# A hybrid attention and ConvFFN layer: TensorE's instructions of the attention stage in written order

## The chip, the cores and the metric

The kernel runs on one core of one Trainium2 chip. The metric is the device time of one execution in microseconds (us). The engines are named as the profile names them: PE is TensorE's matmuls, PEld its weight loads (they overlap the matmuls), DVE is VectorE, ACT is ScalarE, POOL is GpSimd, SP is SyncE, whose queue issues most of the loads.

## The reference

One layer over 256 tokens of width 2048, all in float32. `h @ w_in` gives queries, keys and values for two groups of eight heads of width 128. Eight heads are "forgetting attention" (FoX): normed queries and keys, a softmax over logits with a cumulative forget bias. Eight are "stick-breaking" (SB): weights from a running sum of log-sigmoids. Both results are normed, multiplied by `w_out` and added to x. Then comes an FFN: an up-projection to 2 x 5632 columns, a causal convolution of width 3, a SiLU gate, a down-projection.

```python
def reference(x, attn_norm, w_in, b_forget, q_norm, k_norm, out_norm_fox, out_norm_sb,
              w_out, ffn_norm, w_up, conv_w, conv_b, w_down):
    for layer in range(DEPTH):                       # DEPTH is 1
        h = rms_norm(x, attn_norm[layer])
        x = x + hybrid_mixer(h, w_in[layer], b_forget[layer], q_norm[layer], k_norm[layer],
                             out_norm_fox[layer], out_norm_sb[layer], w_out[layer])
        h = rms_norm(x, ffn_norm[layer])
        x = x + conv_ffn(h, w_up[layer], conv_w[layer], conv_b[layer], w_down[layer])
    return x

# forgetting_attention, per block of queries
        logits = jnp.einsum('bhqd,bhkd->bhqk', qi.astype(jnp.float32), k32) * scale
        logits = logits + ci[..., None] - c32[:, :, None, :]
        ...
        p = jax.nn.softmax(logits, axis=-1)
        return jnp.einsum('bhqk,bhkd->bhqd', p.astype(v.dtype), v)
```

## The kernel before

The arithmetic is float32 made of parts. Each weight tile of 128 x 2048 numbers (1 MB) is loaded into `w_raw` on SP's queue, cast to a rounded part `w_hi` by ACT (L207) and reduced to the rest `w_lo` by DVE (L208, which needs ACT's cast first). Activations are split in the same manner. A product then is three: hi by hi, lo by hi, hi by lo.

In the attention stage the projections to queries, keys and FoX values are cut into weight blocks of four 128-row tiles by up to 512 columns. One block is 24 matmuls in `in_three` (L229): 16 that use `w_hi`, then 8 that use `w_lo`. `w_hi` and `w_lo` have two buffers each in this stage, so that the cast for a block can start when the `w_hi` matmuls of the block two before it have ended, and its `w_lo` split when that block's `w_lo` matmuls have ended.

The heads are Python generators that are advanced by `step()` once after each weight block, at most two heads at a time (`WINDOW = 2`). A FoX head (`fox_head`, L611) goes through these phases:

- four score matmuls into the PSUM tile `ps_s` (L617, L518), then on DVE the bias (L624), the mask (L628) and the row maxima (L630, L631), on ACT the two exponentials (L633, L634), on DVE the reciprocal (L636) and the factors (L637, L638) that make `pr` the softmax weights
- two yields, so two weight blocks, later: `transposed_weights`, three transposes on TensorE into `ps_p` (L603), copied and split by ACT (L606, L607) and DVE (L608) into `pT`
- one yield later: `weighted`, four matmuls into `ps_o` (L589, L590), split into `oT` by ACT (L353) and DVE (L354), with sums of squares (L358, L361, L362)

`ps_s` and `ps_p` share two PSUM buffers. The SB heads are built alike. Queries and keys of four FoX heads pass through `fox_rows`: ACT scales them to `raw` (L298), DVE norms them (L323 to L328), and after one or more yields `to_heads` transposes them into `ps_h` (L304).

What sets the order of instructions: everything inside the attention stage is recorded in the order in which the program writes it, and then a list scheduler, with its own estimates and with priorities (weight loads and splits are written under `high_priority(offset=AHEAD)`), fixes an order for every engine. Two pieces are exempt: the opening (`opening`, the first projection, L473 to L476) and the FFN (from L1090) stand under `tc.manual_schedule`, in which the engines named keep the written order. In both kernels each engine executes its fixed list from front to back, and semaphores hold an instruction until its inputs are there.

The place that matters below is the stretch of the stage in which heads 0 to 3 run beside the last weight block of the queries of heads 4 to 7 (`project(512, 512)`, L648) and the four blocks of their keys (`project(WF + 512 * half, 512)`, L653). The other place is the transpose `pp` of the parameter rows (L128) in `columns(pcol, prow, 50)` (L481), with the small product `gq` (L489) that follows on DVE.

Of the kernel before, what the change touches and what calls it, by code (L numbers as in the profile page):

```python
# [45 lines left out]
def hybrid_layer(  # L46
# [49 lines left out]
    def load_parameters(masks):  # L96
        r0 = KT
        for src, n in (
            (ffn_norm, KT), (out_norm_fox, NH), (out_norm_sb, NH), (q_norm, 1), (k_norm, 1)
        ):  # L100
            nc.sync.dma_start(prow[r0 : r0 + n, :], src[0].rearrange("(n p) -> n p", p=P))
            r0 += n
        nc.sync.dma_start(cs[:, P:], cst[:, P:C_MF])
        nc.sync.dma_start(masks, cst[:, C_MF:])
        nc.sync.dma_start(bf, b_forget.to_broadcast([P, NH]))
# [178 lines left out]
    with ExitStack() as actx:  # L284
# [188 lines left out]
        with tc.high_priority(offset=AHEAD), tc.manual_schedule(  # L473
            engines={mybir.EngineType.PE, mybir.EngineType.DVE, mybir.EngineType.Activation, mybir.EngineType.SP}
        ):
            acc_q0 = opening()  # L476
        masks = at.tile([P, 2 * P], F32, name="masks")
        load_parameters(masks)
        rstd1, _ = token_factors(ss1, 1, diagonal=False)
# [592 lines left out]
    for f_lo, f_hi in FFN_PARTS:  # L1072
# [11 lines left out]
        for g in ORDER if f_hi < NFT else LAST_ORDER:  # L1084
# [7 lines left out]
            engines={mybir.EngineType.PE, mybir.EngineType.DVE, mybir.EngineType.Activation, mybir.EngineType.SP, mybir.EngineType.Pool}  # L1092
# [73 lines left out]
```

## Time and profile before

| | us |
|---|---|
| median of 3 runs | 1104.37 (1104.33 to 1104.72) |
| the profiled execution | 1103.89 |
| its span, first to last instruction | 1102.1 |
| TensorE busy | 1097.4 |
| TensorE weight loads busy | 951.2 |
| DVE busy | 877.1 |
| ACT busy | 700.8 |
| POOL busy | 44.4 |

The granted clock of TensorE is 1.000 over the whole span.

How the rows below are read. A row of the timeline has the start in us, the time from the start of the first to the end of the last instruction of the row, the engine, the line, the operation, the output and inputs, the shape, the count, and in brackets the engine's idle time before it with the instruction that ended it. A row of the waits has the waiting engine and line, what it waited for, the total in us, the times, and the longest. A row of the windows has the stretch, its length, and then for PE, PEld, DVE, ACT and POOL the busy time and the number of instructions, and at the end the granted clock, the share in which the DMA engines were busy and their GB/s. The modelled end of a matmul lies behind the start of the next, so that a group's length is read best from start to start.

### The profile page before, as it was taken

Reading aid. Unit: us, or ns where it says so; the run is one execution under the profiler, and the core shown is the slowest. Engines: PE = TensorE matmul, PEld = TensorE weight load, DVE = VectorE, ACT = ScalarE, POOL = GpSimd, SP = SyncE. Lnnn points to the kernel's source line nnn. Section 1 sums busy time; section 2 is a strip of 40 time slices with the busy share of each in tenths; the row PEclk is TensorE's granted clock in tenths of the full one; section 3 lists DMA queues with packets and bytes.
Section 4 is the critical chain, followed back from the end, with each engine's and each line's share of the span. In section 5 each row is a group of like instructions: output and inputs, shape, how many; then the busy total and the mean of one; then the engine's idle time right before and its main releaser. Section 6 shows DMA issues by size and latency. Waiting matters only on the chain.

```text
span 1102.1 us, 14836 instructions
## 1 busy us (share of the span) xinstructions
PE 1097.4 (100%) x5868; PEld 951.2 (86%) x5868; DVE 877.1 (80%) x941; ACT 700.8 (64%) x879; POOL 44.4 (4%) x46
## 2 busy tenths in 40 slices
PE   9999999999999999999999999999999999999998
PEld 7998888888888888888888888888888888888887
DVE  6656877875775677689889988889798889889896
ACT  6544565664553567667767776767676677667753
POOL 0000000000000000000000010100000010100010
PEclk9999999999999999999999999999999999999999
DMA  8776555475555396558989597987979688987985
GB/s 288 185 233 230 188 154 159 148 253 182 176 168 186 105 326 201 187 170 214 283 229 305 191 238 263 262 267 178 319 207 305 215 219 277 248 265 196 323 213 168
DMA packets 179407, 245.89 MB, mean 223 GB/s; under 512 B 4432, under 2 KB 119018, under 8 KB 179082
## 3 DMA queue, kind: packets, MB, share of 16 engines
q1 hardware_dynamic: 162458, 209.67, 58.4%
q0 software_dynamic: 16560, 34.75, 16.7%
q8 instruction: 46, 0.75, 0.3%
q10 hardware_dynamic: 320, 0.53, 0.1%
q14 instruction: 23, 0.19, 0.0%
HBM read 242.82 MB, written 2.11 MB: 222 GB/s over the span
## 4 chain that ended last, share of the span: by engine, by line
PE 99%; ACT 0%; DVE 0%; issue 0%
PE pu L256 34%; PE acc L229 22%; PE pu L263 18%; PE bank_a L229 10%; PE bank_b L229 5%; PE bank_c L229 2%; PE acc L425 2%; PE acc L1044 1%; PE ps_x L138 1%; PE ps_o L589 1%; PE bank_a L1044 1%; PE ps_p L603 0%; PE ps_o L590 0%; PE ps_h L304 0%; PE idle L378 0%; PE ps_z L518 0%
## 5 line engine op out<-in xcount | busy, mean ns | idle before, releaser
L208 DVE TENSOR_TENSOR w_lo<-w_raw,w_hi 128x2048 fp32r<-128x2048 f32 (+1 forms) x196 | 439.7, 2246 | 148.0 <-ACT w_hi L207 146.8
L207 ACT CAST w_hi<-w_raw 128x2048 fp32r<-128x2048 f32 (+1 forms) x196 | 367.2, 1876 | 265.8 <-PE pu L256 77.1
L256 PE MATMUL pu<-hT,w_hi 128*128 128x512 f32 x1664 | 396.3, 390 | 0.0
L256 PEld LDWEIGHTS pu<-hT,w_hi 128*128 128x128 f32 x1664 | 309.6, 188 | 62.6
L263 PEld LDWEIGHTS pu<-hT,w_lo 128*128 128x128 f32 x1664 | 213.6, 191 | 8.3
L263 PE MATMUL pu<-hT,w_lo 128*128 128x256 f32 x1664 | 216.2, 283 | 0.0
L229 PE MATMUL acc<-w_hi,hT 128*128 128x512 f32 (+1 forms) x576 | 124.9, 368 | 0.0
L229 PEld LDWEIGHTS acc<-w_hi,hT 128*128 128x128 f32 x576 | 101.3, 188 | 14.1
L207 ACT CAST w_hi<-w_sum 128x2048 fp32r<-128x2048 f32 x30 | 57.3, 1909 | 42.8 <-PE pu L256 36.6
L208 DVE TENSOR_TENSOR w_lo<-w_sum,w_hi 128x2048 fp32r<-128x2048 f32 x30 | 68.7, 2290 | 19.3 <-ACT w_hi L207 19.3
L866 ACT ACTIVATE tap<-up,ccol 128x256 f32<-128x256 f32 x176 | 74.6, 495 | 0.0
L229 PE MATMUL acc<-w_lo,hT 128*128 128x512 f32 (+1 forms) x288 | 64.9, 367 | 0.0
L229 PEld LDWEIGHTS acc<-w_lo,hT 128*128 128x128 f32 x288 | 51.6, 188 | 7.4
L971 POOL DMA_DIRECT2D w_sum<-in_w_down_dram x20 | 25.7, 1285 | 796.7 <-DVE w_lo L208 786.1
L229 PE MATMUL acc<-w_hi,oT 128*128 128x512 f32 x192 | 46.0, 392 | 0.0
L229 PEld LDWEIGHTS acc<-w_hi,oT 128*128 128x128 f32 x192 | 35.7, 188 | 7.3
L229 PE MATMUL bank_a<-w_hi,s 128*128 128x512 f32 x160 | 40.1, 392 | 0.1
L229 PE MATMUL bank_b<-w_hi,s 128*128 128x512 f32 x160 | 40.0, 392 | 0.0
L229 PE MATMUL bank_a<-w_hi,g 128*128 128x512 f32 x160 | 40.0, 392 | 0.0
L229 PEld LDWEIGHTS bank_a<-w_hi,s 128*128 128x128 f32 x160 | 28.8, 189 | 5.7 <-issue 0.5
L229 PEld LDWEIGHTS bank_a<-w_hi,g 128*128 128x128 f32 x160 | 28.9, 189 | 5.2
L229 PEld LDWEIGHTS bank_b<-w_hi,s 128*128 128x128 f32 x160 | 28.9, 189 | 5.3
(211 smaller groups left out, 1068.9 us busy)
## 6 DMA issues: line engine op xcount, KB each, us to landing
w_raw<-in_w_up_dram SPq DMA_DIRECT2D x88, 1024.0 KB, 7.6
w_raw<-in_w_down_dram SPq DMA_DIRECT2D x44, 1024.0 KB, 6.5
w_raw<-in_w_in_dram SPq DMA_DIRECT2D x36, 1024.0 KB, 5.3
w_sum<-in_w_down_dram POOLq DMA_DIRECT2D x20, 1024.0 KB, 10.0
w_raw<-in_w_out_dram SPq DMA_DIRECT2D x16, 1024.0 KB, 5.1
w_raw<-in_w_down_dram POOLq DMA_DIRECT2D x10, 1024.0 KB, 14.8
w_raw<-in_w_in_dram SPq DMA_DIRECT2D x12, 688.0 KB, 4.1
w_raw<-in_w_in_dram SPq DMA_DIRECT2D x6, 512.0 KB, 7.7
```

Source lines behind the costliest of these rows:

```text
L138: nc.tensor.transpose(ps[:, j, t * P : (t + 1) * P], xt[t][:, (k + j) * P : (k + j + 1) * P], ident)
L207: act.copy(hi[:, :n], raw[:, :n])
L208: dve.tensor_tensor(lo[:, :n], raw[:, :n], f32(hi[:, :n]), op=ALU.subtract)
L229: nc.tensor.matmul(o, lhs(i, l, t), r[:, i, :], start=starts and j == 0, stop=stops and j == 3 * n - 1, skip_group_check=more,)
L256: nc.tensor.matmul(acc[:, j, :], hi[:, i, j * P : (j + 1) * P], hT[:, k].rearrange("p a b -> p (a b)"), start=k == 0, stop=False,)
L263: nc.tensor.matmul(acc[:, j, S:], lo[:, i, j * P : (j + 1) * P], hT[:, k, 0, :], start=False, stop=k == KT - 1,)
L425: nc.tensor.matmul(acc[:, t, :], of_half(hT[:, 2 * c + i + j], l, t), r[:, j, :], start=high and c == i == m == 0, stop=not high and c == ...
L589: nc.tensor.matmul(po, v[j][:, hs], wp[:, k], start=i == 0, stop=False)
L866: act.activation(taps[w][:, j, :], u[:, j, w : w + S], AF.Copy, scale=ccol[:, w, f : f + 1])
L971: nc.gpsimd.dma_start(mem[into][:, : nk * 512].rearrange("p (a b) -> p a b", a=nk), src, accum_op=ALU.add)
L1044: nc.tensor.matmul(o, of_half(g, l, t), r[:, i, c0 : c0 + cols], start=kh == 0 and j == 0, stop=kh == n - 1 and j == 11,)
```

## The change

One line is added behind the opening. It enters `tc.manual_schedule` for TensorE alone and keeps it until the attention stage closes.

```diff
@@ -474,6 +474,7 @@
             engines={mybir.EngineType.PE, mybir.EngineType.DVE, mybir.EngineType.Activation, mybir.EngineType.SP}
         ):
             acc_q0 = opening()
+        actx.enter_context(tc.manual_schedule(engines={mybir.EngineType.PE}))
         masks = at.tile([P, 2 * P], F32, name="masks")
         load_parameters(masks)
         rstd1, _ = token_factors(ss1, 1, diagonal=False)
```

What TensorE does behind that line keeps the written order among itself, and the scheduler orders the other engines around it. Line numbers behind L476 are one higher in the changed kernel. In the two built programs TensorE's list differs in two places. The transpose `pp` stands behind three instead of two matmuls of the opening's eighth block. And in the stretch named above, where A is the last block of the queries of heads 4 to 7 and B to E are the blocks of their keys:

```
before                                    after
A: 16 w_hi, 8 w_lo                        A: 16 w_hi, 8 w_lo
B: 16 w_hi                                6 ps_p (heads 0 and 1)
1 ps_p                                    B: 16 w_hi, 8 w_lo
B: 1 w_lo                                 8 ps_o (heads 0 and 1)
5 ps_p                                    8 ps_s (heads 2 and 3)
B: 7 w_lo                                 C: 16 w_hi, 8 w_lo
1 ps_o, C: 2 w_hi, 1 ps_o, C: 10 w_hi     8 ps_h
the other 6 ps_o mixed with 8 ps_s        D: 16 w_hi, 8 w_lo
C: 4 w_hi, 8 w_lo                         6 ps_p (heads 2 and 3)
8 ps_h                                    E: 16 w_hi, 8 w_lo
D, 6 ps_p, E
```

ACT's list differs in that stretch alone: the four copies out of `ps_p` (L606, L607 before) now precede the cast for D, and the exponentials of head 2 precede the cast for E. DVE's list differs there too: the two splits of `pT` and the norming of the keys precede the `w_lo` split for D, and some of the work on heads 2 and 3 precedes the split for E. Beside the moved `pp`, DVE's `gq` product stands two instructions later. The lists of POOL and SP are the same.

## The prediction

> **What bounds the kernel now.** I read the page's busy shares and its chain first, then the list of waits of the two TensorE rows (PE matmuls, PEld weight loads), and last the timeline of the one place where the built program of the changed kernel differs.
>
> ```profile
> span 1102.1 us, 14836 instructions
> PE 1097.4 (100%) x5868; PEld 951.2 (86%) x5868; DVE 877.1 (80%) x941; ACT 700.8 (64%) x879; POOL 44.4 (4%) x46
> PE 99%; ACT 0%; DVE 0%; issue 0%
> ```
>
> TensorE is busy for 1097.4 of 1102.1 us and holds 99% of the chain that ends last: a microsecond in which it stands still is a microsecond on the end, unless a later wait of its own gets shorter. So the second view is what there is to get shorter.
>
> ```profile
> PE idle L378 <- DVE zeros L368: 1.1, 1, 1.1
> PE acc L425 <- ACT hT L143: 0.3, 1, 0.3
> ...
> PEld bank_a L229 <- issue: 0.5, 1, 0.5
> ...
> PEld ps_p L603 <- DVE pr L637: 0.3, 1, 0.3
> PEld ps_o L589 <- DVE pT L608: 0.2, 1, 0.2
> PEld ps_o L589 <- ACT pT L606: 0.2, 1, 0.2
> ```
>
> Of TensorE's waits two lie in the opening, before the stage that is changed; behind the changed place only the 0.5 us of bank_a is left. Three small ones (ps_p, ps_o) lie at the changed place itself. The kernel has nothing to win beyond fractions of a microsecond there, and no slack behind it to absorb a loss. DVE and ACT matter only through what they hand to TensorE.
>
> **The change, part by part.** Nothing is computed anew; instructions change places. By the order in which the two built programs stand, TensorE's list differs at two places, DVE's and ACT's at the same two (the scheduler fits them to it), POOL's and SP's queues not at all, so no transfer moves.
>
> First place, near 29 us: the transpose of the parameter rows (pp) stands one 128x512 matmul later, and on DVE the tiny gq product two instructions later.
>
> ```profile
> 28.99 0.26 PE L128 MATMUL pp<-cs,prow 50*128 50x50 f32 x1
> ```
>
> Its reader on DVE copies 50 columns and the next weight split queues behind that copy, one matmul (0.23 us, below) later. TensorE's stream holds the same instructions in either order, so I take nothing; the bounds are 0 and 0.23 us. If that split's cover were gone it would cost those 0.23 us.
>
> Second place, 124 to 136 us, is the case. Call the five weight blocks around it A to E (24 matmuls each: 16 with w_hi, 8 with w_lo): A starts at 118.68 us and ends the queries of FoX heads 4 to 7, B to E are the keys of those heads.
>
> ```profile
> 122.35 1.98 PE L229 MATMUL acc<-w_lo,hT 128*128 128x512 f32 x8
> 124.16 3.79 PE L229 MATMUL acc<-w_hi,hT 128*128 128x512 f32 x16
> 127.81 0.33 PE L603 MATMUL ps_p<-cs,pr 128*128 128x128 f32 x1
> 127.89 0.48 PE L229 MATMUL acc<-w_lo,hT 128*128 128x512 f32 x1
> 128.21 0.76 PE L603 MATMUL ps_p<-cs,pr 128*128 128x128 f32 x5
> 128.72 1.87 PE L229 MATMUL acc<-w_lo,hT 128*128 128x512 f32 x7
> ...
> 138.36 1.03 PE L304 MATMUL ps_h<-cs,raw 128*128 128x128 f32 x8
> ```
>
> Before, the scheduler lets B's 16 w_hi matmuls (124.16 to 127.81) go ahead of the six transposes of the softmax weights of heads 0 and 1 (ps_p, L603), and scatters the products ps_o among B's end and C. In program order all six transposes stand directly behind A, then B whole, then all eight ps_o matmuls and all eight score matmuls ps_s of heads 2 and 3, then C whole. TensorE would reach the first transpose at 124.16 us. When is its input there?
>
> ```profile
> 122.59 1.91 ACT L207 CAST w_hi<-w_raw 128x2048 fp32r<-128x2048 f32 x1
> ...
> 125.29 0.50 ACT L634 ACTIVATE pr<-pr,nm 128x256 f32<-128x256 f32 x1
> ```
>
> ```profile
> 124.54 2.29 DVE L208 TENSOR_TENSOR w_lo<-w_raw,w_hi 128x2048 fp32r<-128x2048 f32 x1 [1.25 <-ACT w_hi L207]
> 126.75 0.22 DVE L636 RECIPROCAL rl<-l 128x2 f32<-128x2 f32 x2
> 126.88 0.67 DVE L323 TENSOR_TENSOR sq<-raw 128x512 f32<-128x512 f32 x1
> 127.47 0.28 DVE L637 TENSOR_SCALAR pr<-pr,rl 128x128 f32<-128x128 f32 x1
> 127.67 0.35 DVE L638 TENSOR_SCALAR pr<-pr,rl 128x256 f32<-128x256 f32 x1
> 127.93 0.28 DVE L637 TENSOR_SCALAR pr<-pr,rl 128x128 f32<-128x128 f32 x1
> 128.12 0.35 DVE L638 TENSOR_SCALAR pr<-pr,rl 128x256 f32<-128x256 f32 x1
> ```
>
> The last factor is applied at 127.47 to 128.47 us (L637, L638), behind a weight split of 2.29 us that itself waited for ACT's cast. Up to these four instructions the order of DVE and of ACT from 30 us on is the same in both programs, and nothing in it waits for B. So the inputs come when they came: the first transpose starts at 127.81, the sixth follows head 1's last factor, and the next matmul starts at 128.72, as before. The difference is what is left to do at 128.72: before, seven w_lo matmuls of B; now, all 24 of B.
>
> The sum, from the start of B before (124.16) to the start of E before (145.28), by stretches of the trace:
>
> ```profile
> 117.53:118.68 1.15, 1.15 (x11) 1.15 (x10) 0.82 (x1) 0.29 (x1) 0.00 (x0) 1.00 0.55 210
> 118.68:124.16 5.48, 5.48 (x26) 4.51 (x25) 4.57 (x11) 2.06 (x3) 0.00 (x0) 1.00 0.52 166
> 124.16:145.28 21.12, 21.12 (x114) 17.54 (x112) 19.40 (x48) 14.54 (x35) 0.00 (x0) 1.00 0.50 152
> 139.15:144.71 5.56, 5.56 (x28) 4.54 (x27) 4.58 (x11) 4.16 (x9) 0.00 (x0) 1.00 0.46 132
> 144.71:145.28 0.57, 0.57 (x8) 0.57 (x6) 0.25 (x1) 0.34 (x2) 0.00 (x0) 1.00 1.08 370
> 150.85:151.93 1.08, 1.08 (x11) 1.07 (x10) 0.70 (x1) 1.08 (x3) 0.00 (x0) 1.00 1.04 361
> ```
>
> Each stretch is one undisturbed group: 1.15 us for eight ps_s, 5.48 for a block (0.23 a matmul), 5.56 for D, 0.57 for six ps_p, 1.08 for eight ps_o; the eight ps_h take 0.79 (138.36 to 139.15). Work after: from 128.72 on B 5.48 + ps_o 1.08 + ps_s 1.15 + C 5.48 + ps_h 0.79 + D 5.56 + ps_p 0.57 = 20.11, so E starts at 148.83 instead of 145.28: **3.55 us later**. The same seen as waits: 124.16 to 128.72 is 4.56 us for transposes of 0.57, a stall of 3.99; the scattered order before lost 21.12 - (20.11 + 0.57) = 0.44 us to its small waits, which the program order wins back.
>
> Does a second wait follow? The queue behind the waiting transposes is all of TensorE; what waits for it is the freeing of weight buffers, thus the splits for D and E on ACT and DVE, and behind DVE's split the chain of heads 2 and 3.
>
> ```profile
> 134.73 0.48 DVE L354 SCALAR_TENSOR_TENSOR oT<-ps_o,pcol,oT 128x256 fp32r<-128x256 f32 x1
> ...
> 136.13 0.73 DVE L624 SCALAR_TENSOR_TENSOR pr<-minus_c,c_of,ps_s 128x128 f32<-128x128 f32 x2
> ...
> 143.49 0.35 DVE L638 TENSOR_SCALAR pr<-pr,rl 128x256 f32<-128x256 f32 x1
> ```
>
> B's w_hi part ends at 128.72 + 3.79 = 132.51; ACT's cast for D (1.91) ends at 134.42, DVE's split (2.29) at 136.71, two oT instructions (0.48 each) at 137.67. From first score add to last factor the chain of heads 2 and 3 took 136.13 to 143.84, 7.71 us with E's split in it; from 137.67 it ends at 145.38. TensorE wants it at 148.83 - 0.57 = 148.26: 2.9 us of cover. D wants its split at 142.7 and has it at 136.7. Behind E the orders are equal, so I take nothing more. If this cover were gone, the cost is its overrun; I bound it by 1 us.
>
> The profiled execution took 1103.89 us, 1.79 outside its span; the median of the runs is 1104.37, 0.48 above it. 1104.37 + 3.55 = **1107.9 us**, slower by 0.32%.
>
> **Rivals.** *The stall makes TensorE slow.* Between A's last matmul (122.35 + 1.98 = 124.33) and the first transpose lie 3.48 us of silence, 4.39 up to B's first matmul. What a TensorE does that comes out of idleness is seen at the kernel's start:
>
> ```profile
> 2.73 1.06 PE L378 MATMUL idle<-zeros 128*128 128x256 bf16 x4
> 5.03 0.60 PE L378 MATMUL idle<-zeros 128*128 128x256 bf16 x4
> L378 PE MATMUL idle<-zeros x18: 272/421/421, 1.1 to 5.4; 128*128 128x256 bf16 x18
> 2.00:3.00 1.00, 1.00 (x7) 0.69 (x6) 0.00 (x0) 0.50 (x1) 0.00 (x0) 1.00 0.71 201
> ```
>
> The same matmul of zeros first comes every (1.06 - 0.42) / 3 = 0.21 us, and every (0.60 - 0.27) / 3 = 0.11 us from 5.03 us on: half speed for some 3.9 us after the first at 1.1, while the granted clock reads 1.00. If the silence brings that back, B's first 3.9 us do half their work and 2.0 us are added: 1109.9. [...] Against it: the silence is barely as long as the half-speed stretch at the start, and no later row of the list of waits is long enough to show it. [...] I give it 0.17.
>
> *The other side: no change.* If the factors were there when TensorE comes, at 124.16, the program order would even win its 0.44 us: 1103.9. The mechanism would be DVE taking the reciprocals and factors ahead of the split at 124.54. It decides from a first factor 2 us earlier than 127.47, where the loss falls under 2.2 us. But the exponentials end on ACT only at 125.79, and the built program keeps the split first. I give 0.07 to this and to a TensorE that does not keep the written order, and 0.03 to a gain of over 0.2% from anything unseen.
>
> *A second stall.* The cover of 2.9 us for heads 2 and 3 is worked out, not seen. An overrun of up to 1 us gives 1108.9. I give it 0.05.
>
> **How the numbers follow.** 0.2% of the median, 2.2 us, is about what a measurement of this kernel can tell from no change. Forecast 0.68 (its own range 1107.4 to 1108.4: 3.55 less the 0.5 us of bank_a that a later wait might give back, or plus the 0.44 if the small waits stay), slow TensorE 0.17, second stall 0.05: slower 0.90. No change 0.07, faster 0.03. The range goes from 1107.2, the forecast's lower bound and 0.2 for the profiled row against the median, to 1110.0, which takes in the half-speed case; it leaves out the 0.10 below.
>
> **What would show it.** In the profile after: the list of waits gets one row of about 3.6 us for the weight loads or matmuls of ps_p on DVE's pr, at 124 to 128 us, once, and the ps_o waits go. B's first matmul starts near 128.7, C's near 136.4, E's near 148.8, and every later block some 3.5 us later than before, to a span near 1105.6. ps_p of heads 2 and 3 shows no wait. Half speed would show as B's matmuls every 0.46 us for up to 3.9 us instead of 0.23. The prediction is wrong if the first transpose starts well before 127.8, if B runs slowly, or if a wait over 0.5 us stands anywhere behind E that is not there now.

## The result

| | before | after |
|---|---|---|
| median of 6 runs each, us | 1104.31 (1104.0 to 1104.72) | 1109.22 (1108.26 to 1110.43) |
| the profiled execution, us | 1103.89 | 1110.43 |
| its span, us | 1102.1 | 1108.6 |

The changed kernel is slower by 4.9 us: a ratio of 1.0045 with a 95% interval of 1.0035 to 1.0055. The forecast was 1107.9 us, the range 1107.2 to 1110.0. Its direction, place and main term hold. The forecast took TensorE at full speed behind the wait, and that did not come true: the granted clock over the span is 0.998 in each of the six runs, where the profiled execution of the kernel before has 1.000.

The profiled execution is the slowest of the six, so its 6.5 us over the span before are more than the median's 4.9. First the list of waits of TensorE's matmuls in the changed kernel (what waited for what; total, times, longest in us), whose line numbers are one higher than before:

```profile
PE ps_p L604 <- DVE pr L638: 3.5, 1, 3.5
PE bank_a L229 <- ACT w_hi L207: 1.1, 1, 1.1
PE idle L378 <- DVE zeros L368: 1.1, 1, 1.1
PE acc L425 <- DVE w_hi L406: 0.7, 1, 0.7
```

The row of 3.5 us is the predicted one. The small waits on ps_o are gone. The others are not the change's: acc lies in the opening at 6 us (0.3 before), and bank_a lies at 1086 us in the last FFN part; over the executions traced for this study it varies from nothing to 1.8 us, and it is 0.9 us in a run below whose time equals the kernel before.

The timeline of the place in TensorE's matmuls, with the end of A, the transposes, B and the start of E:

```profile
119.20 3.83 PE L229 MATMUL acc<-w_hi,hT 128*128 128x512 f32 x16
122.86 1.98 PE L229 MATMUL acc<-w_lo,hT 128*128 128x512 f32 x8
128.31 1.59 PE L604 MATMUL ps_p<-cs,pr 128*128 128x128 f32 x6 [3.48 <-DVE pr L638]
129.56 4.71 PE L229 MATMUL acc<-w_hi,hT 128*128 128x512 f32 x16
134.11 1.98 PE L229 MATMUL acc<-w_lo,hT 128*128 128x512 f32 x8
...
150.06 0.82 PE L604 MATMUL ps_p<-cs,pr 128*128 128x128 f32 x6
150.63 3.92 PE L229 MATMUL acc<-w_hi,hT 128*128 128x512 f32 x16
```

A starts 0.52 us later than before (119.20 against 118.68, from the opening). From the start of A to the start of E it is 31.43 us against 145.28 - 118.68 = 26.60 before: 4.83 us are lost here. The rest to 6.5 is the 0.52 ahead of A and 1.1 on bank_a. Of the rows, the transposes take 129.56 - 128.31 = 1.25 us where 0.91 was forecast from the row before, and B's w_hi part takes 134.11 - 129.56 = 4.55 us where it took 3.65 (3.75 in the kernel with the silence filled, below). The stretches of that time show why; the third number from the right is the granted clock:

```profile
126.00:127.00 1.00, 0.00 (x0) 0.00 (x0) 1.00 (x1) 1.00 (x4) 0.00 (x0) 1.00 0.00 0
127.00:128.00 1.00, 0.00 (x0) 0.00 (x0) 1.00 (x5) 0.54 (x1) 0.00 (x0) 0.93 0.00 0
128.00:129.00 1.00, 0.69 (x3) 0.61 (x4) 1.00 (x6) 0.00 (x0) 0.00 (x0) 0.50 0.67 84
...
130.00:131.00 1.00, 1.00 (x4) 0.71 (x4) 1.00 (x4) 0.79 (x4) 0.00 (x0) 0.50 1.08 385
131.00:132.00 1.00, 1.00 (x5) 0.87 (x4) 0.97 (x7) 0.21 (x2) 0.00 (x0) 0.87 0.96 329
132.00:133.00 1.00, 1.00 (x6) 0.79 (x6) 0.93 (x4) 0.20 (x1) 0.00 (x0) 1.00 0.02 6
```

The clock is halved from about 127.86 us on, still in the silence, to about 131.26 us. In a mean of 0.93 over 1 us, 2 x 0.07 = 0.14 us are at half speed; with 3 us at 0.50 and 2 x 0.13 = 0.26 that makes 3.40 us, of which 2.95 lie behind the first transpose. DVE's first factor for these transposes (first row below) came when it was forecast, 8.78 us behind A's start (8.79 before), and the next chain, of heads 2 and 3 (second row), had cover:

```profile
127.98 0.28 DVE L638 TENSOR_SCALAR pr<-pr,rl 128x128 f32<-128x128 f32 x1
...
147.18 0.35 DVE L639 TENSOR_SCALAR pr<-pr,rl 128x256 f32<-128x256 f32 x1
```

The second row ended at 147.53 and was wanted at 150.06: 2.5 us, where 2.9 were worked out.

### The profile page after: what moved, and what is told of

The parts are those of the page before. It is cut to its first block, busy times and chain, and to the rows that moved or that the text cites. A ratio compares the mean times of both kernels' runs of the same rounds, so it can differ in the third digit from the quotient of the medians.

```text
span 1108.6 us, 14836 instructions
## 1 busy us (share of the span) xinstructions
PE 1099.0 (99%) x5868; PEld 952.6 (86%) x5868; DVE 877.1 (79%) x941; ACT 701.2 (63%) x879; POOL 44.4 (4%) x46
```

## The experiments

All kernels keep the changed kernel's line unless their edit says otherwise. Times are compared with runs of the kernel before that were taken beside them: 1104.94 us for the first four, 1104.20 us for the next four, 1104.84 us (one run) for the last four. The granted clock is known for every run, the timeline for the profiled one alone.

**The silence filled.** In `fox_head`, ahead of the transposes:

```diff
             yield
             yield
+            if h == 0:
+                fill = psb.tile([P, S], F32, name="fill", tag="t")
+                for _ in range(28):
+                    nc.tensor.matmul(fill, zeros[:, :P], zeros, start=True, stop=True)
             w = transposed_weights(pr, "pT")
```

> Edit: 28 matmuls of zeros (128x256, bf16) into a spare PSUM tile are written between block A and the six transposes of heads 0 and 1; nothing reads them. They take 28 x 0.11 = 3.1 us and end before the factors are there, so that TensorE's order behind them and the wait for the factors stay as in the changed kernel, but its silence shrinks from 3.5 us to about 0.4 us. Theory (the loss is the wait for the factors, 3.55 us net, and about 1.3 us of half speed behind the silence): the granted clock stays 1.00 from 125 to 135 us, B's matmuls come every 0.23 us at once, 1104.3 + 3.55 = 1107.9 us. Rival (the loss beyond 3.55 us comes from waits elsewhere, not from the clock): the time stays at 1109.2 us whatever the clock does.

Measured: 1108.15 us (1107.95 to 1108.76, 8 runs), ratio 1.0027 (1.0017 to 1.0037), clock 1.000 in all eight. The theory's signs came: the clock stayed up and the time fell below the 1109.2 us of the rival. Its timeline:

```profile
118.83 3.83 PE L229 MATMUL acc<-w_hi,hT 128*128 128x512 f32 x16
...
124.31 3.23 PE L645 MATMUL fill<-zeros 128*128 128x256 bf16 x28
127.95 1.16 PE L604 MATMUL ps_p<-cs,pr 128*128 128x128 f32 x6 [0.41 <-DVE pr L638]
128.86 3.90 PE L229 MATMUL acc<-w_hi,hT 128*128 128x512 f32 x16
...
149.14 3.92 PE L229 MATMUL acc<-w_hi,hT 128*128 128x512 f32 x16
```

With 28 useless matmuls more, A to E takes 30.31 us, 1.12 less than in the changed kernel. The transposes come 3.64 us after they could, as without the filling, take 0.91 us, and B runs at full speed. So 30.31 - 26.60 = 3.71 us are the wait (3.55 were forecast), and the other 1.12 of the profiled execution are the clock: 1.25 - 0.91 = 0.34 on the transposes and 4.55 - 3.75 = 0.80 on B's w_hi part. (The medians differ by 3.2 us, less than these 3.71; waits elsewhere, such as bank_a, vary by more than that difference.) The lists of the other engines are the same as in the changed kernel.

**Filled in part.** The same edit with 12 instead of 28, which leaves a silence of 2.2 us.

> Edit: as with 28, but 12 matmuls of zeros, 1.3 us, at the front of the wait; a silence of about 2.2 us is left ahead of the transposes. In the changed kernel the clock fell 3.0 us after the end of A's last matmul. Theory with a threshold in the length of the silence: no fall, clock 1.00, 1107.9 us as with 28. Rival (any stall of some 2 us halves the clock, or a low share of busy time does): the clock shows 0.50 near the transposes and the time lies between 1108.3 and 1109.2 us.

Measured: 1109.81 us (five runs: 1108.03, 1108.46, 1109.81, 1109.92, 1110.02), ratio 1.0037 (1.0023 to 1.0051). The lower two have a clock of 1.000, the upper three of 0.998; the profiled run is one of the lower two (1108.46, no fall). Neither expectation covers two groups. The theory of a threshold in the length of the silence is out, since the same edit gave both clocks; the rival's fall came in three of five runs, at times above its 1109.2 us.

**The heads not advanced by the projections' own steps.** The order is kept, the stall taken away.

```diff
     def step():
+        step_waiting()
+        step_heads()
+
+    def step_waiting():
         for g in list(waiting)[:WINDOW]:
             if next(g, g) is g:
                 waiting.remove(g)
+
+    def step_heads():
         stepped = 0
...
                 waiting.append(fox_rows(project(512, 512), qT, gq))
-                step()
+                step_waiting()
...
             waiting.append(fox_rows(project(WF + 512 * half, 512), kT, g_k))
-            step()
+            step_waiting()
```

> Edit: TensorE keeps the written order as in the changed kernel, but the two step() calls that follow the making of a fox_rows generator for heads 4 to 7 advance only the projections, not the heads. The transposes of heads 0 and 1 are then written behind block B instead of A, 5.5 us later than the place where they had to wait 3.9 us for the factors; their ps_o stands behind C, and heads 2 and 3 follow one block later. Theory (the written order costs nothing by itself, only the one stall does): no wait for the factors, clock 1.000, 1104.3 less the 0.44 us of small waits of the kernel before: 1103.9 us, at most 1104.4. Rival (the written order as such, or the other engines' lists fitted to it, costs time): over 1106 us, with new waits in the list.

Measured: 1106.72 us (11 runs, 1105.92 to 1110.04), ratio 1.0016 (1.0007 to 1.0025). The wait on ps_p is gone, and the clock is 1.000 in nine runs, 0.999 in one and 0.998 in the slowest (1110.04), whose timeline is not known, so that the place of its fall stays open. The theory misses. The rival's signs came, over 1106 us and new waits in the list, but not for its reason, as the kernel with `fox_rows(..., 3)` below shows: the edit made waits of its own.

```profile
PE bank_a L235 <- ACT w_hi L213: 1.8, 1, 1.8
PE ps_o L596 <- DVE low L316: 1.1, 1, 1.1
PE idle L384 <- DVE zeros L374: 1.1, 1, 1.1
PE ps_o L596 <- ACT qA L314: 0.3, 1, 0.3
```

The transposes of the queries (ps_h) now stood directly in front of ps_o, in the two PSUM buffers that both use, and ps_o waited 1.4 us until ACT and DVE had read them.

**The first place alone.** The written order is entered at L477 and left before the first queries (L520).

> Edit: the written order is kept for TensorE only from behind the opening to the first queries, so that of the change only its first place is left: the transpose of the parameter rows one matmul later, and gq two instructions later on DVE. Theory: nothing, 1104.3 us, at most 0.23 us more. Rival (part of the loss of 4.9 us is made here, by a later weight split): 1105 us or more.

Measured: 1104.86 us (11 runs), ratio 0.9997 (0.9988 to 1.0006). The moved pp costs nothing that can be told.

**The changed kernel again.**

> The changed kernel once more, beside the kernels of this call. Theory: 4.7 to 4.9 us over the kernel before; from the start of A to the start of E about 4.8 us longer than before (3.7 with the silence filled, 1.1 for the half speed); the clock falls to 0.50 about 3.0 us after A's last matmul ends, in a place that does not move, since it fell in all runs so far. [...]

Measured: 1109.65 us (5 runs, 1109.08 to 1111.1), ratio 1.005 (1.0038 to 1.0063), clock 0.998 in all five. That is 5.45 us over the kernel before, more than the 4.7 to 4.9 expected, and the fall did not stay in its place.

```profile
119.09 3.83 PE L229 MATMUL acc<-w_hi,hT 128*128 128x512 f32 x16
...
128.21 1.16 PE L604 MATMUL ps_p<-cs,pr 128*128 128x128 f32 x6 [3.48 <-DVE pr L638]
129.12 5.50 PE L229 MATMUL acc<-w_hi,hT 128*128 128x512 f32 x16
134.46 1.98 PE L229 MATMUL acc<-w_lo,hT 128*128 128x512 f32 x8
...
150.98 3.92 PE L229 MATMUL acc<-w_hi,hT 128*128 128x512 f32 x16
```

```profile
128.00:129.00 1.00, 0.79 (x5) 0.55 (x6) 1.00 (x5) 0.06 (x1) 0.00 (x0) 1.00 0.59 94
129.00:130.00 1.00, 1.00 (x6) 0.85 (x6) 1.00 (x3) 0.94 (x4) 0.00 (x0) 0.78 0.94 265
...
132.00:133.00 1.00, 1.00 (x4) 0.81 (x3) 0.93 (x4) 0.09 (x1) 0.00 (x0) 0.51 0.00 1
133.00:134.00 1.00, 1.00 (x5) 0.80 (x5) 0.93 (x3) 0.00 (x0) 0.00 (x0) 1.00 0.00 0
```

The transposes ran at full speed, and the clock fell at 129.56 us, 1.35 us after TensorE had resumed, again for 3.42 us (0.44 + 2 + 0.98). All of it lay on work: A to E took 31.89 us, 1.58 over the filled kernel.

**The heads' own steps, and the queries' transposes a block later.** The edit of the third experiment, and in addition

```diff
-                waiting.append(fox_rows(project(512, 512), qT, gq))
+                waiting.append(fox_rows(project(512, 512), qT, gq, 3))
```

> Edit: as the own_step kernel, and the queries of heads 4 to 7 are transposed (ps_h) one block later, so that ps_h no longer stands in front of ps_o and holds its PSUM buffers, which cost 1.4 us there. Theory: no wait of TensorE from A to the SB heads; from A to E the work of the kernel before less its 0.44 us of small waits; the time equals the kernel before within 0.1%, 0.4 us less if that can be told. Rival (the written order costs by itself): 1.5 us or more over the kernel before.

Measured: 1104.19 us against 1104.20 (11 runs, 1103.61 to 1106.72), ratio 1.0 (0.9991 to 1.0009), clock 1.000 in the profiled run. In its whole list of TensorE's matmul waits one row is left; the rows of the timeline behind it are the start of A and the first matmul behind E and its six transposes:

```profile
PE idle L384 <- DVE zeros L374: 1.1, 1, 1.1
```

```profile
118.86 3.83 PE L235 MATMUL acc<-w_hi,hT 128*128 128x512 f32 x16
...
150.64 3.92 PE L262 MATMUL pu<-hT,w_hi 128*128 128x512 f32 x16
```

The written order as such costs nothing; the order is good where what it puts next is ready. From the start of A to there the trace has 150.64 - 118.86 = 31.78 us, against 150.85 - 118.68 = 32.17 for the same matmuls before, so 0.39 of the 0.44 us of small waits are won back there; in the time of the whole kernel they cannot be told from nothing.

**A silence of 3.0 us.** The filling with 4 matmuls.

> Edit: 4 matmuls of zeros (0.45 us) in front of the wait; a silence of about 3.0 us is left. Theory with a threshold near 3.0 us after the last matmul: borderline, the clock falls as the transposes begin or not at all; without a fall 3.6 us over the kernel before, with one 4.5 to 5. [...]

Measured: 1109.22 us (five runs: 1107.84, 1108.01, 1109.22, 1109.58, 1109.85), ratio 1.0042 (1.003 to 1.0055). The profiled run (1108.01) has a wait of 3.0 us on ps_p and no fall. There are two groups again: the lower two at a clock of 1.000, the upper three at 0.998.

**A longer silence.** In `fox_head`, ahead of the reciprocal:

```diff
+            for _ in range(12 if h == 0 else 0):
+                dve.tensor_scalar(l, l, 1.0, None, op0=ALU.mult)
             rl = small.tile([P, NT], F32, name="rl", tag="rl")
```

> Edit: twelve small DVE instructions that multiply head 0's sums by 1 stand ahead of its reciprocal, each behind the other, so that DVE's chain to the factors takes 4 to 6 us longer and TensorE's silence grows from 3.5 to 8 or 9 us. Theory: the added silence is added to the time one for one, and the half speed adds no more than the 2.0 us taken from the kernel's start, since only the stretch behind the silence counts: 1104.3 + 3.55 + 5 + 2.0 = 1114.9 us, within 1.5 us. Rival (the other engines' lists swallow part of a longer wait, because later stages have slack): under 1112 us.

Measured: 1114.68 us (4 runs, 1113.85 to 1115.68), ratio 1.0095 (1.0081 to 1.0109), clock 0.995 in three runs and 0.997 in the fastest.

```profile
119.26 3.83 PE L229 MATMUL acc<-w_hi,hT 128*128 128x512 f32 x16
...
133.26 1.59 PE L604 MATMUL ps_p<-cs,pr 128*128 128x128 f32 x6 [8.36 <-DVE pr L640]
134.50 6.17 PE L229 MATMUL acc<-w_hi,hT 128*128 128x512 f32 x16
...
157.05 3.92 PE L229 MATMUL acc<-w_hi,hT 128*128 128x512 f32 x16
```

```profile
129.00:130.00 1.00, 0.00 (x0) 0.00 (x0) 1.00 (x4) 0.00 (x0) 0.00 (x0) 0.56 0.83 231
...
138.00:139.00 1.00, 1.00 (x4) 0.74 (x3) 0.00 (x0) 0.00 (x0) 0.00 (x0) 0.50 0.00 0
139.00:140.00 1.00, 1.00 (x5) 0.81 (x4) 0.00 (x0) 0.00 (x0) 0.00 (x0) 0.82 0.00 0
```

The silence grew by 8.36 - 3.48 = 4.88 us and came out whole in the time; nothing behind it gave any of it back, and the rival (under 1112 us) is out. A to E is 37.79 us: 30.31 + 4.88 + 2.60 for the clock, more than the 2.0 that I had set as its most. The rows give the clock's part by themselves: over the filled kernel, 0.33 on the transposes (1.24 against 0.91) and 2.26 on B's w_hi part (6.01 against 3.75). The half speed lasted 0.88 + 9 + 0.36 = 10.24 us, three times the 3.40 and 3.42 us of the two traces of the changed kernel.

**Four more traced executions**, three with 12 matmuls of zeros, one with 4, to see whether the clock falls in those at the upper times.

> The kernel with 12 matmuls of zeros, one look at its clock. Five runs of it lay at 1108.0 to 1108.5 and at 1109.8 to 1110.0 us, and only one of the lower ones left a trace (no fall of the clock). [...]

> [...]

> [...]

> The kernel with 4 matmuls of zeros, a silence of 3.0 us, one more look at its clock. Five runs of it lay at 1107.8 to 1108.0 and at 1109.2 to 1109.9 us; the trace of a lower one shows no fall. [...]

Measured, with 12: 1108.44 us at clock 1.000, A to E 30.32 us; 1109.67 us at 0.998, A to E 31.75 us; 1109.55 us at 0.998, A to E 31.68 us. With 4: 1111.0 us at 0.998, A to E 31.77 us, and a wait of 1.0 us on bank_a. In the three executions with a fall, A to E is 1.4 to 1.5 us longer than without one (30.32 us with 12 and with 4). The wait on bank_a does not make the upper times: with 12 it was 0.7 us in the lowest of the three and 0.4 and none in the others. The rows of the second with 12:

```profile
119.02 3.83 PE L229 MATMUL acc<-w_hi,hT 128*128 128x512 f32 x16
...
124.50 1.48 PE L645 MATMUL fill<-zeros 128*128 128x256 bf16 x12
128.14 1.59 PE L604 MATMUL ps_p<-cs,pr 128*128 128x128 f32 x6 [2.15 <-DVE pr L638]
...
150.77 3.92 PE L229 MATMUL acc<-w_hi,hT 128*128 128x512 f32 x16
```

```profile
127.00:128.00 1.00, 0.00 (x0) 0.00 (x0) 1.00 (x5) 0.36 (x1) 0.00 (x0) 1.00 0.00 0
128.00:129.00 1.00, 0.86 (x4) 0.74 (x5) 1.00 (x5) 0.00 (x0) 0.00 (x0) 0.65 0.71 75
...
131.00:132.00 1.00, 1.00 (x5) 0.76 (x4) 0.93 (x7) 0.38 (x2) 0.00 (x0) 0.64 0.93 313
```

With a silence of 2.15 us the fall came at 128.30 us and lasted 0.70 + 2 + 0.72 = 3.42 us, and the 3.4 us before it held 1.1 us of matmuls of zeros. The silence is 2.15 or 2.16 us in all four traced executions with 12, two with a fall and two without. The clock of every run settles the two groups: of the 14 executions with 12 or 4 matmuls, the five at 1.000 lie at 1107.84 to 1108.46 us and the nine at 0.998 at 1109.22 to 1111.0. Why the same silence brings a fall in one execution and none in another, the runs do not show.

## Why the prediction was right, and where it was off

- The measured 1109.22 us lies inside the range of 1107.2 to 1110.0 only because the range took in the half-speed case. The forecast's own range without it, 1107.4 to 1108.4, does not reach it, and one of the prediction's own signs of being wrong came: B ran slowly. B started at 129.56 us for 128.7 and E at 150.63 for 148.8.
- *What bounds the kernel* holds. The longer wait came out in the time one for one, with no slack behind it, and the kernel without the stall is where the kernel before is.
- *The first place, pp, at nothing:* right, measured alone at a ratio of 0.9997.
- *The wait for the factors.* Right in place, releaser and size: 3.64 us from the first moment to the first transpose (3.65 forecast), 3.71 us net from A to E with the clock kept up (3.55 forecast; the stretch from B to E took 20.28 instead of 20.11 us).
- *No second stall:* right. ps_p of heads 2 and 3 shows no wait, with 2.5 us of cover. (The 142.7 us at which D is said to want its split is D's start; its w_lo matmuls come 3.74 us later, so that this cover was larger than written.)
- *The rival "The stall makes TensorE slow", at 0.17*, is the step that failed. It was no rival but a term of the sum, which the forecast put at nothing: the clock was 0.998 in all eleven runs of the changed kernel, the six of the result and the five beside the experiments. The argument against it set the silence of 3.48 us beside the half-speed stretch of 3.9 us at the start; that a silence has to be that long was not shown. The clock fell in 5 of 8 executions with a silence of 2.15 us, and in the one shown the 3.4 us ahead of the fall held 1.1 us of matmuls of zeros. The term was sized at 2.0 us from the kernel's start; it measured 1.1 and 1.6 us in the two traces of the changed kernel. With 3.71 that makes 4.8 to 5.3 us, and the medians say 4.9 and 5.45.
- *The place of the fall* is not explained by the runs. In the changed kernel it came 3.0 us after A's end in one trace and 4.8 us in the other, there at 129.56 us, after 1.35 us of renewed work. The half-speed stretches lasted 3.40 to 3.42 us in five traces and 10.24 us in one.
- *The change does what it says*, and the side of "no change" needed factors that came 2 us earlier; they came as forecast.

The chapter on the kernel before says that two yields are two weight blocks. That is not so here, and it is the reason why just these transposes came too early. Between the scores and the transposes lie two yields, but for heads 0 and 1 not two weight blocks: the `step()` that follows the making of the queries' generator (L649) advances the heads once more, without a block in between. They had one block, A, of 5.5 us for a chain that, from the first score matmul to the last factor, took 128.47 - 117.53 = 10.9 us in the trace before. Heads 2 and 3 had C and D. The scheduler had covered this by letting B's w_hi matmuls go first.

## What to carry to other kernels

When an engine that bounds the kernel is put into written order, look for each instruction whose input comes later than its place, and price it as its lateness: here 3.64 us at the transposes came out as 3.71 us, and 4.88 us more as 4.88. For TensorE add to a stall of the sizes seen here the half speed that may follow it, here 1.1 to 1.6 us for 2.2 to 3.5 us of silence and 2.6 us for 8.4. The cure is to write the instruction behind work that is ready, after seeing what buffers it then shares with its new neighbours.

## What the runs showed of the hardware that was not expected

Near a silence of TensorE its granted clock fell to 0.50. By the clock of every run, this came in none of 8 executions with a silence of 0.4 us, in 5 of 8 with 2.15 us, in 4 of 6 with 3.0 us, in all 11 of the changed kernel with 3.5 us, and in all 4 with 8.4 us. The half speed lasted 3.40 to 3.42 us in five traces, and its start differed: in one it began 0.45 us before TensorE resumed, in another 1.35 us after. After 8.4 us of silence it took 139.36 - 133.26 = 6.1 us of work, the first 1.24 us of it transposes, until full speed was back.
